# The start of a fused transformer block: g_mix_pre first, the first weights in pieces, and zeros through TensorE until they are there

## The chip, the cores and the metric

One core of one Trainium2 chip runs the whole kernel. The metric is the device time in microseconds (us) of one execution, the median over runs.

## The reference, cut to what matters

One layer of a hybrid block on `x` of 1024 tokens by 1024 channels, all in float32:

```python
h = rmsnorm(x, g_mix_pre)                       # x * rsqrt(mean(x*x) + eps) * g
proj = h @ w_in                                 # 1024 x 3592
qa, ka, va, gate_a, beta_a, alpha_a, qb, kb, vb = split(proj)
out_a = gated_deltanet(qa, ka, va, gate_a, beta_a, alpha_a, ...)
out_b = dilated_attention(qb, kb, vb, rel_bias)
x = x + rmsnorm(concat(out_a, out_b) @ w_out, g_mix_post)
h = rmsnorm(x, g_ffn_pre)
x = x + rmsnorm((silu(h @ w_gate) * (h @ w_up)) @ w_down, g_ffn_post)
```

The change lies in the loads and the first products of `proj = h @ w_in`. The kernel multiplies `x * g` by the weights and puts the factor `rsqrt(mean(x*x) + eps)` of a token on the result.

## The kernel before, in words

Every float32 matrix operand is split in two: a rounded high part `hi` (float32r, cast by ScalarE) and the rest `lo = x - hi` (VectorE). A product is three matmuls (`mm3`): hi by hi, hi by lo, lo by hi. Names that end in `h` and `l` (`hTh`, `hTl`) are these two parts.

The work is written as strands: Python generators that yield one operation after the other. A planner (`Weaver`) picks at each step the operation that its own cost table lets start first, and so writes out one fixed order for each engine before the chip sees anything. On the chip each engine keeps its order and waits on semaphores. So a change in what a strand yields, or in when the planner believes data to be there, can move other instructions. An `After` request makes a strand wait in the planner's clock until the tile was written; a `Get` waits for a free buffer.

The part at issue, in the program's order:

- **Weights.** `load_w` issues loads on SyncE's queue (SP). `w_in` lies in 128-column chunks; a chunk goes to two tiles `wr` of four k tiles each (256 KB). Four buffers `wr` exist. `prep_w` casts and subtracts (`split_sb`) each to tiles `w`.
- **x, transposed.** `load_xt(k, hf)` loads 128 channels (k tile k of 8) by 512 tokens (half hf) to `xT` (256 KB, six buffers); `prep_xt` multiplies by the column of `gT` (the transposed `g_mix_pre`, 4 KB) on ScalarE (`hTh`) and VectorE (`hTl`).
- **x, by tokens.** `load_x(t)` loads 128 tokens by 1024 channels to `xn` (512 KB, three buffers). `norm_in` sums the squares on ScalarE (the instruction that writes `junk`), then VectorE (`n_m`) and GpSimd (`rtok`) make the factor of each token. The fourth `xn` load needs the buffer of the first, and so waits for the first sum of squares; the eighth waits for the fifth's. For every four token tiles, four TensorE transposes against `ident` turn `rtok` into a row, which ScalarE copies to `rb`. The fourth of these transposes needs the fourth `rtok`.
- **TensorE.** `main` runs `proj_first(hf)`, 48 matmuls of 128x512 (8 k tiles, two chunks: `k0` and `q0` in the list `ORDER`, three each) into two banks `pj`, and then `proj_v(0, ...)` for four token tiles: 24 matmuls of 128x264 each into banks `tp`. First hf = 0 with token tiles 0 to 3, then hf = 1 with 4 to 7, then the next chunks (`proj_half`).

Loads leave SP in this order: weights and xT of half 0, `wba`, the four tiles for `proj_v`, `ident`, four `xn`, eight `xT` of half 1, four more `xn`, further weights.

Of the kernel before, what the change touches and what calls it, by code (L numbers as in the profile page):

```python
# [11 lines left out]
F32 = mybir.dt.float32  # L12
# [200 lines left out]
class After:  # L213


    def __init__(self, *aps, late=0.0):
        self.aps, self.late = aps, late


class Strand:  # L220
# [16 lines left out]
class Weaver:  # L237
# [125 lines left out]
    def run(self, *until):  # L363
        while not all(e.set for e in until):
            live, moved = [], True
            while moved:
                moved, live = False, []
                for s in list(self.strands):
                    old = s.req
                    if self.step(s):  # L370
                        live.append(s)
                    if s.req is not old:
                        moved = True
                if self.fresh:
                    self.fresh, moved = False, True
            if all(e.set for e in until):
                break
            assert live, [(s.gen.__name__, s.gen.gi_frame.f_lineno, s.req.__class__.__name__) for s in self.strands]
            first = 1e30
            for s in live:  # L380
                if s.alts is not None:
                    s.req = s.alts[0]
                    if s.ver >= 0:
                        s.req = min(s.alts, key=lambda r: self.finish(s, r, live))
                names = [x.tensor.name for x in s.req.aps] if isinstance(s.req, After) else \
                    [x[0] for op in s.req for x in op.ins + op.outs]
                v = sum(self.ver.get(n, 0) for n in names)
                if v != s.ver:
                    s.ver = v
                    if isinstance(s.req, After):  # L390
                        s.data = max([t for x in s.req.aps for t, _ in self.wr.get(x.tensor.name, {}).values()] + [0.0])
                    else:
                        s.data = max(self.when(op) for op in s.req)
                if isinstance(s.req, After):
                    s.start, s.safe = s.data + s.req.late, True
                else:
                    free = self.clock[s.req[0].eng]
                    s.start = max(free, s.data, self.port if s.req[0].port else 0.0)
                    if s.req[0].eng == "PE":
                        s.start = max(s.start, self.rest.get(s.gen.__name__, 0.0) if s.pace else 0.0)  # L400
                    if s.req[0].table not in (None, self.table) and not s.eager:
                        s.start += TABLE
                    s.safe = s.req[0].eng != "PE" or s.data + s.slack <= free
                first = min(first, s.start)
            best = min((s for s in live if s.start == first), key=lambda s: s.prio)
            if isinstance(best.req, After):
                best.req = None
                continue
            eng = best.req[0].eng
            same = [s for s in live if not isinstance(s.req, After) and s.req[0].eng == eng]  # L410
            best = min((s for s in same if s.start <= first), key=lambda s: (not s.safe, s.prio))
            start = best.start
            if best.req[0].table is not None:
                start = best.data
            for op in best.req:
                start = max(start, self.clock[eng])
                self.issue(op, start)
            if best.pace and eng == "PE":
                self.rest[best.gen.__name__] = self.clock[eng] + best.pace
            best.req = None  # L420
# [121 lines left out]
def block_kernel(ctx: ExitStack, tc: tile.TileContext, a, out):  # L542
# [23 lines left out]
    def split_sb(hi, lo, src):  # L566
        yield Either(A.copy(hi, src), V.tensor_copy(hi, src), bias=BIAS)
        yield Either(*[e.tensor_tensor(lo, src, hi.bitcast(F32), ALU.subtract) for e in (V, G)])
# [77 lines left out]
    def chunks(item):  # L646
        kind, i = item
        return [24 + 2 * i, 25 + 2 * i] if kind == "bv" else [base[kind] + i]
# [3 lines left out]

    def load_w():

        first = chunks(order[0]) + chunks(order[1])
        got = {c: [] for c in first}
        evs = {c: [Event() for _ in range(2)] for c in first}
        for i in range(2):
            for n, c in enumerate(first):
                wr = yield rawS.get([P, 4, P], F32, name="wr")  # L660
                yield SY.dma_start(wr[:], a["w_in"][c][:, 4 * i:4 * i + 4, :])
                got[c].append(wr)
                evs[c][i].fire()
                if not i:
                    w.spawn(prep_w(c, got[c], evs[c]), 1)
                yield from load_xt(4 * i + n, 0)
                if not i and not n:
                    yield SY.dma_start(gT[:], a["g_mix_pre_t"])
            for k in (2, 3):
                yield from load_xt(4 * i + k, 0)  # L670
        yield SY.dma_start(wba[:], a["w_ba"])
        yield from load_item(order[2])
        yield SY.dma_start(ident[:], a["c_ident"])
        for t in range(4):
            yield from load_x(t)
        for k in range(KT):
            yield from load_xt(k, 1)
        for t in range(4, NT):
            yield from load_x(t)
        ev_x.fire()  # L680
        for item in order[3:]:
            yield from load_item(item)

    def load_item(item):
        for c in chunks(item):
            z, evs = [], [Event() for _ in range(2)]
            for i in range(2):
                wr = yield rawS.get([P, 4, P], F32, name="wr")
                yield SY.dma_start(wr[:], a["w_in"][c][:, 4 * i:4 * i + 4, :])
                z.append(wr)  # L690
                evs[i].fire()
            w.spawn(prep_w(c, z, evs), 1)

    ev_x = Event()
    ev_wh = {(c, i): Event() for c in loaded for i in range(2)}

    def prep_w(c, raw, got):
        hi, lo = [], []
        for i in range(4):
            if c in (24, 25):  # L700
                z = yield wS.get([P, 2, WB], F32R, name="w")
            else:
                z = yield wS.get([P, 4, P], F32R, name="w")
            (lo if i % 2 else hi).append(z)
        wts[c] = hi, lo
        for i, (wh, wl) in enumerate(zip(hi, lo)):
            yield got[i]
            wr = raw[i]
            if c in (24, 25):

                k = 4 * (c - 24) + 2 * i
                yield After(wba[:])
                yield from split_sb(wh[:, :, 256:], wl[:, :, 256:], wba[:, k:k + 2, :])
                wh, wl, wx = wh[:, :, 0:256], wl[:, :, 0:256], wr[:].rearrange("p (k x) c -> p k (x c)", x=2)
            else:
                wh, wl, wx = wh[:], wl[:], wr[:]
            yield After(wr[:])
            yield from split_sb(wh, wl, wx)
            rawS.put(wr)
            ev_wh[c, i].fire()  # L720
        loaded[c].fire()

    def proj_first(hf, sinks):

        cs = chunks(order[0]) + chunks(order[1])
        ps = []
        for _ in cs:
            z = yield pj.get([P, 512], F32, name="pj")
            ps.append(z)
        for k in range(KT):  # L730
            for c, z in zip(cs, ps):
                yield ev_wh[c, k // 4]
                yield ev_xt[k, hf]
                wh, wl = wts[c]
                yield mm3(z[:], wh[k // 4][:, k % 4, :], wl[k // 4][:, k % 4, :], *h_of(k, hf * 512, 512),
                          k == 0, k == KT - 1)
        if hf:
            wS.slots = wS.slots[:8]
            for c in cs:
                wS.put(*wts[c][0], *wts[c][1])  # L740
        return [w.spawn(sink(hf, z), 1) for sink, z in zip(sinks, ps)]
# [554 lines left out]
    with ExitStack() as s0:  # L1296
# [10 lines left out]
        def prep_xt(k, hf, x):  # L1307
# [5 lines left out]
            px.put(x)  # L1313
            ev_xt[k, hf].fire()

        def load_x(t):
            x = yield px.get([P, D], F32, name="xn", bufs=3)
            yield SY.dma_start(x[:], a["x"][t * P:(t + 1) * P, :])
            done_in.append(w.spawn(norm_in(t, x), 1))

        def norm_in(t, x):
# [7 lines left out]
            if t % 4 == 3:  # L1329
# [6 lines left out]
                pt.put(tp)  # L1336
                ev_rb[t // 4].fire()

        w.spawn(issue(V.memset(mhalf[:], -0.5)), 0)
        wS.more(px, "pw", 8)  # L1340
        w.spawn(load_w(), 2)
# [1110 lines left out]
```

## Time and profile before

| | us |
|---|---|
| median of 3 runs | 1224.42 (1222.09 to 1224.97) |
| profiled execution | 1225.21, span 1223.4 |
| TensorE busy | 1203.1 (98% of the span) |
| VectorE, ScalarE, GpSimd busy | 884.5, 546.3, 157.3 |
| first real matmul starts | 5.82 |
| first 48 matmuls (half 0) end and `proj_v` begins | 20.16 |
| half 1 begins, ends | 32.25, 43.13 |
| third group of 128x512 matmuls begins | 55.62 |

Starts are counted from the start of the span; 1.8 us of the profiled execution's own time lie outside the span. In a timeline row the first number is the start, the second the length (of several instructions in a row together), and the bracket says how long the engine stood idle and what ended that. A matmul's length holds its way through the array, so two neighbours overlap; the distance of starts is what one costs. `SPq` rows are DMA issues on SyncE's queue: their length holds the time that the queue waited before it could issue.

### The profile page before, as it was taken

To read this page: it belongs to the slowest core of one execution; us is meant where nothing else is said; L and a number is where in the kernel's file an instruction comes from. 1 tells how busy PE (TensorE), PEld (TensorE's weight loads), DVE (VectorE), ACT (ScalarE), POOL (GpSimd) and SP (SyncE) were. 2 spreads that over 40 slices of the span, in tenths; PEclk is the share of its full clock that TensorE was granted. 3 is DMA by queue.
4 is the path that set the end of the run, shared out by engine and by line. 5 is a ranking of instruction groups with operands and counts; after the bars stand their busy time and mean duration, and the time that the engine had idled before them with its cause. 6 is when DMAs were issued, how large, how long until landed. Compare 5 with 4: busy or idle time off the path is not lost.

```text
span 1223.4 us, 19593 instructions
## 1 busy us (share of the span) xinstructions
PE 1203.1 (98%) x7135; PEld 998.1 (82%) x7135; DVE 884.5 (72%) x1627; ACT 546.3 (45%) x1063; POOL 157.3 (13%) x138
## 2 busy tenths in 40 slices
PE   8999999999999999899999999999999999999997
PEld 6878798788888778788788888888888888888886
DVE  4689969646665756666998876877668767876886
ACT  6655521226665654454643323333333334544541
POOL 0143411001111100001100110111001100000111
PEclk9999999999999999899999999999999999999999
DMA  7655363667546355674544433322343239645335
GB/s 266 207 148 168 104 181 105 135 230 243 188 148 208 106 169 170 217 231 146 183 154 139 138 112 130 120 82 83 104 129 121 74 108 321 229 138 147 103 121 206
DMA packets 152887, 193.03 MB, mean 158 GB/s; under 512 B 29992, under 2 KB 78376, under 8 KB 152792
## 3 DMA queue, kind: packets, MB, share of 16 engines
q1 hardware_dynamic: 148568, 189.69, 48.2%
q10 hardware_dynamic: 4224, 2.10, 0.6%
q8 instruction: 56, 0.92, 0.3%
q14 instruction: 39, 0.32, 0.1%
HBM read 135.88 MB, written 59.66 MB: 160 GB/s over the span
## 4 chain that ended last, share of the span: by engine, by line
PE 83%; DMA 5%; DVE 5%; ACT 2%; issue 2%; SPq 1%; POOL 1%; DVEq 0%; POOLq 0%; ACTq 0%
PE bank L286 47%; PE pj L286 21%; PE tp L286 4%; PE p L286 3%; PE pw L286 3%; PE pS L286 2%; PE pV L286 2%; PE pm L286 2%; DVE yc L286 1%; DMA xn<-in_x 1%; SPq L286 1%; DMA h2l<-d_h 1%; DVE x L286 1%; ACT junk L286 1%; DMA views<-in_w_down 0%
## 5 line engine op out<-in xcount | busy, mean ns | idle before, releaser
L286 PE MATMUL pj<-hTh,w 128*128 128x512 f32 x768 | 264.1, 405 | 5.8 <-ACT hTh L286 5.8
L286 PEld LDWEIGHTS pj<-hTh,w 128*128 128x128 f32 x768 | 145.5, 189 | 40.5 <-ACT hTh L286 5.8
L286 ACT CAST wbh<-wraw 128x512 fp32r<-128x512 f32 x130 | 80.3, 621 | 199.0 <-PE bank L286 123.8
L286 PE MATMUL pj<-hTl,w 128*128 128x512 f32 x384 | 151.2, 394 | 0.0
L286 DVE TENSOR_TENSOR wbl<-wraw,wbh 128x512 fp32r<-128x512 f32 x131 | 92.2, 706 | 29.2 <-ACT wbh L286 29.0
L286 PE MATMUL bank<-views 128*128 128x512 f32 (+1 forms) x307 | 84.8, 384 | 0.0
L286 PEld LDWEIGHTS pj<-hTl,w 128*128 128x128 f32 x384 | 73.0, 190 | 12.6 <-DVE hTl L286 0.7
L286 PE MATMUL bank<-views,dah 128*128 128x512 f32 (+1 forms) x214 | 73.5, 379 | 0.0
L286 PE MATMUL bank<-dbh,views 128*128 128x512 f32 (+1 forms) x201 | 70.3, 380 | 0.0
L286 PEld LDWEIGHTS bank<-views 128*128 128x128 f32 x307 | 57.5, 188 | 11.4
L286 POOL TENSOR_TENSOR m<-m,m 128x512 f32<-128x512 f32 x18 | 28.3, 1573 | 253.2 <-DVE r L286 179.6
L286 PE MATMUL pw<-woh,mh 128*128 128x512 f32 x128 | 52.9, 413 | 3.5 <-ACT mh L286 3.4
L286 ACT CAST w<-wr 128x512 fp32r<-128x512 f32 x53 | 32.5, 617 | 52.2 <-PE pj L286 46.8
L286 PE MATMUL pw<-woh,ml 128*128 128x512 f32 x128 | 51.0, 398 | 0.0
L286 PE MATMUL pw<-wol,mh 128*128 128x512 f32 x128 | 50.9, 398 | 0.0
L286 PE MATMUL bank<-dbh,dah 128*128 128x512 f32 (+1 forms) x129 | 49.1, 381 | 0.0
L286 DVE TENSOR_TENSOR w<-wr,w 128x512 fp32r<-128x512 f32 x44 | 30.6, 702 | 24.9 <-ACT w L286 23.3
L286 DVE SCALAR_TENSOR_TENSOR yc<-raw,convw,yc 128x1024 f32<-128x1024 f32 x36 | 46.5, 1292 | 0.5
L286 PEld LDWEIGHTS bank<-views,dah 128*128 128x128 f32 x214 | 40.0, 188 | 7.7
L286 PEld LDWEIGHTS bank<-dbh,views 128*128 128x128 f32 x201 | 37.7, 188 | 7.1
L286 DVE TENSOR_TENSOR m<-bank,m 128x512 f32<-128x512 f32 x44 | 30.1, 685 | 18.1 <-PE bank L286 18.0
L286 ACT ACTIVATE Sr<-Sr,mx 128x384 f32<-128x384 f32 (+3 forms) x64 | 38.1, 597 | 6.3 <-DVE mx L286 5.9
(377 smaller groups left out, 3058.1 us busy)
## 6 DMA issues: line engine op xcount, KB each, us to landing
wr<-in_w_in SPq DMA_DIRECT2D x56, 256.0 KB
wraw<-in_w_gate SPq DMA_DIRECT2D x52, 256.0 KB
wraw<-in_w_up SPq DMA_DIRECT2D x52, 256.0 KB
views<-d_hid SPq DMA_DIRECT2D x47, 256.0 KB
db<-in_w_down SPq DMA_DIRECT2D x40, 256.0 KB
da<-d_hid SPq DMA_DIRECT2D x30, 256.0 KB
d_hid<-x SPq DMA_DIRECT2D x22, 256.0 KB
d_hid<-r SPq DMA_DIRECT2D x22, 256.0 KB
```

What stands on the lines that cost most here:

```text
L286: op.fn(*op.args, **op.kw)
```

## The change

`load_w` loads `gT` before all else. For the two first chunks a weight tile is loaded in two pieces of two k tiles (128 KB each), in the order: k0 piece, xT, q0 piece, xT, and again for each two k tiles. `prep_w` casts and subtracts by piece; there is one event per piece, and `proj_first` waits for the piece that it needs. `After` can look at a part of a tile. A new strand `warm` clears half of `junk` on VectorE and runs ten matmuls of bf16 zeros, 128x512, into a `tp` bank that is given back.

```diff
     def load_w():
 
+        yield SY.dma_start(gT[:], a["g_mix_pre_t"])
         first = chunks(order[0]) + chunks(order[1])
         got = {c: [] for c in first}
-        evs = {c: [Event() for _ in range(2)] for c in first}
-        for i in range(2):
+        evs = {c: [[Event() for _ in range(2)] for _ in range(2)] for c in first}
+        for k in range(0, KT, 2):
+            i, j = k // 4, k % 4
             for n, c in enumerate(first):
-                wr = yield rawS.get([P, 4, P], F32, name="wr")
-                yield SY.dma_start(wr[:], a["w_in"][c][:, 4 * i:4 * i + 4, :])
-                got[c].append(wr)
-                evs[c][i].fire()
-                if not i:
+                if not j:
+                    wr = yield rawS.get([P, 4, P], F32, name="wr")
+                    got[c].append(wr)
+                yield SY.dma_start(got[c][i][:, j:j + 2, :], a["w_in"][c][:, k:k + 2, :])
+                evs[c][i][j // 2].fire()
+                if not k:
                     w.spawn(prep_w(c, got[c], evs[c]), 1)
-                yield from load_xt(4 * i + n, 0)
-                if not i and not n:
-                    yield SY.dma_start(gT[:], a["g_mix_pre_t"])
-            for k in (2, 3):
-                yield from load_xt(4 * i + k, 0)
+                yield from load_xt(k + n, 0)
...
     def prep_w(c, raw, got):
...
-            yield After(wr[:])
-            yield from split_sb(wh, wl, wx)
+            for j, ev in enumerate(got[i]):
+                yield ev
+                x = (slice(None), slice(2 * j, 2 * j + 2) if len(got[i]) > 1 else slice(None))
+                yield After(wx[x], part=len(got[i]) > 1)
+                yield from split_sb(wh[x], wl[x], wx[x])
+                ev_wh[c, 2 * i + j].fire()
             rawS.put(wr)
-            ev_wh[c, i].fire()
...
-                yield ev_wh[c, k // 4]
+                yield ev_wh[c, k // 2]
...
+        def warm():
+            yield V.memset(junk[:, 0:512], 0.0)
+            tp = yield pt.get([P, 4, P], F32, name="tp")
+            yield [mm(tp[:].rearrange("p k j -> p (k j)"), junk[:, 0:P], junk[:, 0:512]) for _ in range(10)]
+            pt.put(tp)
...
+        w.spawn(warm(), 0)
         w.spawn(issue(V.memset(mhalf[:], -0.5)), 0)
```

Since the planner sees other times, it also writes other orders for the first part of the program. Behind that part the orders are the same but for the numbers in names. Three places of the new orders:

SP at the very start, before:

```order
L286 DMA wr<-in_w_in 128x512
L286 DMA xT<-in_x_t 128x512
L286 DMA gT<-in_g_mix_pre_t 128x8
L286 DMA wr<-in_w_in 128x512
L286 DMA xT<-in_x_t 128x512 x3
```

and after (`128x8` is `gT`, `128x256` a piece of a weight tile):

```order
L286 DMA gT<-in_g_mix_pre_t 128x8
L286 DMA wr<-in_w_in 128x256
L286 DMA xT<-in_x_t 128x512
L286 DMA wr<-in_w_in 128x256
L286 DMA xT<-in_x_t 128x512
```

`gT` moved from third to first, and a piece of each chunk stands ahead of each two x tiles' second.

ScalarE where half 0 ends, before (`ss0` to `ss3` are the sums of squares of token tiles 0 to 3, `raw<-pj` the copies out of the two banks of half 0):

```order
L286 COPY raw_149<-pj_157 128x512
L286 CAST w_252<-wr_244 128x2x256
L286 COPY raw_150<-pj_158 128x512
L286 ACTIVATE junk_155,ss0_268<-xn_260 128x1024
L286 ACTIVATE junk_155,ss1_274<-xn_267 128x1024
L286 ACTIVATE vs_340<-tp_311,rtok_96 128x256
L286 ACTIVATE bp_129<-tp_311,rtok_96 128x8
L286 ACTIVATE junk_155,ss2_279<-xn_273 128x1024
L286 ACTIVATE vs_387<-tp_339,rtok_96 128x256
L286 ACTIVATE junk_155,ss3_345<-xn_326 128x1024
```

and after:

```order
L286 CAST w_277<-wr_270 128x2x256
L286 ACTIVATE junk_155,ss0_292<-xn_286 128x1024
L286 COPY raw_149<-pj_156 128x512
L286 ACTIVATE junk_155,ss1_298<-xn_291 128x1024
L286 COPY raw_150<-pj_157 128x512
L286 ACTIVATE junk_155,ss2_306<-xn_297 128x1024
L286 ACTIVATE junk_155,ss3_339<-xn_328 128x1024
L286 ACTIVATE hTh_108<-xT_338,gT_154 128x512
L286 ACTIVATE hTh_108<-xT_344,gT_154 128x512
L286 ACTIVATE vs_383<-tp_336,rtok_96 128x256
```

The first sum of squares moved ahead of the first copy out of a bank, and all four ahead of the first `vs`.

TensorE around the second group of transposes of `rtok`, before (`pj` rows belong to half 1, `tp` rows to `proj_v` of token tile 4):

```order
L286 MATMUL pj_479<-hTl_111,w_175 128x512
L286 MATMUL pj_479<-hTh_110,w_176 128x512
...
L286 MATMUL tp_578<-w_231,hTh_108 128x264
L286 MATMUL tp_578<-w_232,hTh_108 128x264
L286 MATMUL tp_578<-w_231,hTl_109 128x264
L286 MATMUL tp_592<-ident_66,rtok_96 128x128 x4
L286 MATMUL tp_578<-w_250,hTh_110 128x264
```

and after:

```order
L286 MATMUL pj_515<-hTh_110,w_169 128x512
L286 MATMUL pj_515<-hTl_111,w_169 128x512
L286 MATMUL pj_515<-hTh_110,w_170 128x512
L286 MATMUL tp_587<-ident_66,rtok_96 128x128 x4
L286 MATMUL pj_516<-hTh_110,w_187 128x512
...
L286 MATMUL pj_516<-hTh_110,w_188 128x512
L286 MATMUL tp_614<-w_247,hTh_108 128x264
```

These transposes moved from behind the 12th matmul of token tile 4 to behind the 39th of the 48 matmuls of half 1, so 21 matmuls earlier. The first group moved as well: it stood behind 78 of the 96 matmuls of `proj_v` for token tiles 0 to 3, and stands behind 54 of them now.

More of the change, by code (lines that the diff above doesn't have):

```diff
@@ L213, with __init__ @@
 class After:
-    def __init__(self, *aps, late=0.0):
-        self.aps, self.late = aps, late
+    def __init__(self, *aps, late=0.0, part=False):
+        self.aps, self.late, self.part = aps, late, part
 class Strand:
@@ L390, in run @@
                     if isinstance(s.req, After):
-                        s.data = max([t for x in s.req.aps for t, _ in self.wr.get(x.tensor.name, {}).values()] + [0.0])
+                        own = [self.region(x) if s.req.part else (x.tensor.name, -1, -1) for x in s.req.aps]
+                        s.data = max([t for n, q, f in own for (p, g), (t, _) in self.wr.get(n, {}).items() if p & q and f & g] + [0.0])
                     else:
@@ L685, in load_item @@
         for c in chunks(item):
-            z, evs = [], [Event() for _ in range(2)]
+            z, evs = [], [[Event()] for _ in range(2)]
             for i in range(2):
@@ L690, in load_item @@
                 z.append(wr)
-                evs[i].fire()
+                evs[i][0].fire()
             w.spawn(prep_w(c, z, evs), 1)
     ev_x = Event()
-    ev_wh = {(c, i): Event() for c in loaded for i in range(2)}
+    ev_wh = {(c, i): Event() for c in loaded for i in range(4)}
     def prep_w(c, raw, got):
@@ L706, in prep_w @@
         for i, (wh, wl) in enumerate(zip(hi, lo)):
-            yield got[i]
+            yield got[i][0]
             wr = raw[i]
```

## The prediction

> **What bounds the kernel now.** The page gives TensorE 98% of the span. I then read TensorE's waits over the whole kernel; only 20 us are idle, and the groups that matter here are these (wait, total, times, longest).
>
> ```profile
> PE 1203.1 (98%) x7135; PEld 998.1 (82%) x7135; DVE 884.5 (72%) x1627; ACT 546.3 (45%) x1063; POOL 157.3 (13%) x138
> ...
> PE pj L286 <- ACT hTh L286: 5.8, 1, 5.8
> PE pw L286 <- ACT mh L286: 3.4, 1, 3.4
> ...
> PE pm L286 <- DVE rhd L286: 1.0, 1, 1.0
> ...
> PE tp L286 <- POOL rtok L286: 0.2, 1, 0.2
> ```
>
> The 5.8 us wait is the start. The timeline shows what it waits for, and a second loss that counts as busy: TensorE is slow at first.
>
> ```profile
> 0.74 0.40 SPq L286 DMA_DIRECT2D wr<-in_w_in  x1
> 1.20 0.41 SPq L286 DMA_DIRECT2D xT<-in_x_t  x1
> 1.65 0.43 SPq L286 DMA_DIRECT2D gT<-in_g_mix_pre_t  x1
> ...
> 3.48 0.62 ACT L286 CAST w<-wr 128x512 fp32r<-128x512 f32 x1 [1.46 <-DMA wr<-in_w_in]
> ...
> 5.04 0.72 ACT L286 ACTIVATE hTh<-xT,gT 128x512 fp32r<-128x512 f32 x1 [0.95 <-DMA gT<-in_g_mix_pre_t]
> ...
> 5.82 0.80 PE L286 MATMUL pj<-hTh,w 128*128 128x512 f32 x1 [5.82 <-ACT hTh L286]
> ...
> 10.05 1.05 PE L286 MATMUL pj<-hTh,w 128*128 128x512 f32 x2
> 10.91 0.63 PE L286 MATMUL pj<-hTl,w 128*128 128x512 f32 x1
> ...
> 19.25 0.62 PE L286 MATMUL pj<-hTh,w 128*128 128x512 f32 x2
> 19.70 0.39 PE L286 MATMUL pj<-hTl,w 128*128 128x512 f32 x1
> ...
> 20.16 0.41 PE L286 MATMUL tp<-w,hTh 128*128 128x264 f32 x2
> ...
> 29.62 0.60 PE L286 MATMUL tp<-ident,rtok 128*128 128x128 f32 x4
> ...
> 32.25 0.39 PE L286 MATMUL pj<-hTh,w 128*128 128x512 f32 x1
> ...
> 43.13 0.41 PE L286 MATMUL tp<-w,hTh 128*128 128x264 f32 x2
> ...
> 45.26 0.32 PE L286 MATMUL tp<-ident,rtok 128*128 128x128 f32 x1 [0.17 <-POOL rtok L286]
> 45.34 0.49 PE L286 MATMUL tp<-w,hTh 128*128 128x264 f32 x2
> ...
> 55.62 0.39 PE L286 MATMUL pj<-hTh,w 128*128 128x512 f32 x1
> ...
> 152.45 0.73 PE L286 MATMUL pm<-rhd,tgtr 128*128 128x512 f32 x2 [0.99 <-DVE rhd L286]
> ```
>
> Two starts of 128x512 are 0.86 us apart at 10.05 (0.43 each) and 0.45 us apart at 19.25 (0.23 each). So the 48 matmuls of half 0 take 14.34 us (5.82 to 20.16), while the same 48 of half 1 take 10.88 (32.25 to 43.13; 0.227 each): 3.46 us are lost to the slow clock and to gaps. A 128x264 costs 9.46 / 78 = 0.121 (20.16 to 29.62) or 10.28 / 84 = 0.122 (45.34 to 55.62).
>
> The row at 45.26 is the important one. TensorE waits only 0.17 us there for the eighth `rtok`, but it waits: something else arrives at the same time as TensorE. The chain of waits up to there names it.
>
> ```profile
> 21.16 1.17 ACT junk L286 x2
> ...
> 22.34 0.33 SPq L286
> ...
> 22.71 5.41 DMA xT<-in_x_t
> ...
> 28.15 1.39 ACT hTh L286 x2
> ...
> 29.57 0.75 DVE hTl L286
> ...
> 30.72 6.49 DMA xn<-in_x
> ...
> 37.30 1.16 ACT junk L286 x2
> ...
> 38.47 4.62 DMA xn<-in_x
> ...
> 44.66 0.56 POOL rtok L286
> ...
> 45.26 10.52 PE tp L286 x85
> ```
>
> It is a chain of loads: the first sum of squares (21.16) frees the `xn` buffer for the fourth load (22.34); behind it the xT loads of half 1 go, the last two of which wait for `hTl`; then the fifth `xn` (30.72), whose sum of squares frees the buffer of the eighth (38.47), whose `rtok` TensorE needs. No TensorE work is in it from 21.16 on. From the first sum of squares to the second transposes' end of waiting it is 45.26 - 21.16 = 24.10 us.
>
> **The change, part by part.**
>
> *gT first, pieces.* gT leaves first, so it is no longer last at 5.04; xT is issued third, at about 1.65. Its landing is between 2.7 us after issue (first weight tile, 0.74 to 3.48) and 3.3 (gT, 1.65 to 5.0): 4.4 to 5.0, so the first real matmul could start 0.78 later, at 5.2 to 5.8. Four casts and four subtractions more fall on ScalarE and VectorE; between no cost (the data is the same) and 8 x 0.62, they lie beside a TensorE that needs 10.9 us for what these engines do in less, and cost nothing; without that cover the last k tile would be late by them.
>
> *Ten zero matmuls.* At the slow 0.43 they take 4.3 us. The clear is short and VectorE idle, so they run from about 1.4 to 5.7, in TensorE's 5.8 us of idleness, and the real ones start at about 5.7. What they are worth is the clock: between nothing (14.34 stays) and all of 3.46. I take 0.8 us left over, since the release need not coincide with 5.7 and the data come one k tile at a time: half 0 ends at 5.7 + 10.88 + 0.8 = 17.4 instead of 20.16, 2.8 earlier. [...]
>
> *Reordered transposes.* Here the gain meets the chain of loads. ScalarE's first sum of squares stood behind the copy out of the bank that TensorE fills last, hence 21.16. Now it stands ahead of it and waits for its load alone. When does that land? These rows bound it.
>
> ```profile
> 13.32 9.35 SPq L286 DMA_DIRECT2D xn<-in_x  x4
> ...
> 16.50:20.00 3.50, 3.50 (x17) 2.88 (x16) 1.20 (x3) 0.74 (x3) 0.00 (x0) 1.00 0.89 325
> 20.00:22.00 2.00, 2.00 (x18) 1.96 (x17) 0.69 (x1) 2.00 (x4) 0.00 (x0) 1.00 0.14 57
> ...
> 26.61 1.05 ACT L286 ACTIVATE junk<-xn 128x1024 bf16<-128x1024 f32 x1
> ...
> 28.02 0.55 POOL L286 TENSOR_TENSOR rtok<-n_m,mhalf 128x1 f32<-128x1 f32 x1 [2.15 <-DVE n_m L286]
> ```
>
> The queue is full up to 20 (last columns: DMA share, GB/s), and 1.5 MB at 325 GB/s are 4.7 us: three `xn` loads move from about 15.4 to 20, the first third until 17.0; but the row of 20 to 22 shows a tail of 2 us, for a load has landed only with its slowest engine. So 17.0 to 20; I take 19.4, near the upper end, for every `xn` here has that tail. The bytes ahead of it are the same as before, so it does not come sooner because TensorE does. The chain moves from 21.16 to 19.45, by 1.7 us.
>
> First transposes: the fourth `rtok` ended at 28.57 and comes at 26.9 at the latest; since the sum at 26.61 had also stood behind a `vs`, I take 26.6. TensorE arrives at 17.4 + 54 x 0.121 = 23.9 and waits 2.7 us. Then 0.36 for the transposes and 42 x 0.121 bring half 1 to 32.05, against 32.25: the lead is gone.
>
> Second transposes: TensorE arrives at 32.05 + 39 x 0.227 = 40.9. The release is 45.26 - 1.7, less 0.33 for one store (`d_v`) that no longer stands between the loads: 43.2. It waits 2.3 us. Behind the transposes there are now 9 x 0.227 + 96 x 0.122 = 13.8 us of work, where 84 x 0.122 = 10.3 stood: the third group begins at 43.2 + 0.08 + 13.8 = 57.1 against 55.62, so 1.5 us later.
>
> *What comes after.* The orders behind are the same and TensorE is busy, so the 1.5 us travel on. VectorE gets `rb` earlier (43.3 against 45.3 for the transposes), so the one wait for VectorE, 0.99 us at 152.45, goes: 0.5 us are left. The wait for `mh` hangs on stores and loads behind TensorE's work and moves along.
>
> Sum against the profiled execution: 1225.21 + 0.5 = 1225.7. That execution lies 0.79 above the median of 1224.42, so in terms of medians: **1224.9 us**.
>
> **The rivals.**
>
> *The loads come in time.* If no engine had a tail, the first `xn` would land at 17.0 and every later load up to 2 us sooner; TensorE would not wait and the third group would begin 17.4 + 35.46 = 52.9, 2.8 us earlier: 1221.7. For it: tails differ from run to run. Against it: the chain has four such loads in a row and must lose 5 us, not 2. And VectorE, which ends the wait at 152.45, would have to come forward as well.
>
> *The clock falls again in the new wait (slower).* One row shows what a long wait does: TensorE idles from 493.8, and the granted clock (PEclk) is half for 6.8 us.
>
> ```profile
> 493.80:496.90 3.10, 0.42 (x2) 0.00 (x0) 3.09 (x5) 1.65 (x5) 0.40 (x1) 1.00 0.75 234
> 496.90:503.70 6.80, 6.09 (x16) 4.83 (x17) 3.02 (x6) 1.24 (x4) 0.56 (x1) 0.50 0.58 165
> ```
>
> Half a clock for the 6.1 busy us costs 3.0. At the first transposes this would be half hidden (2.3 us of slack before the second). At the second nothing hides it: if that wait grows from 2.3 to the 3.4 us of this row, the time is 0.5 + 1.1 + 3.0 = 4.6 over: 1229. It decides at 1.1 us more tail. [...]
>
> *The zeros do not lift the clock.* Half 0 would end at about 20, TensorE would reach the first transposes at 26.5, just when they are released, and all that follows is as forecast: 1224.9. The forecast does not need the lift.
>
> **How the numbers follow.** About 0.3% (3.7 us) is what a measurement of this kernel tells from no change. Forecast (a small loss, hidden gain) 0.62, zeros without effect 0.08 (same time), loads in time 0.20, clock falls 0.10. Loads in time reaches below 1220.7 in a third of its cases, and other clock waits spread by a few us, so faster by over 0.3%: 0.09; slower 0.13 with the tails of the forecast; within 0.78. The range leaves out the slow rival and the lower half of the fast one: 1221.2 to 1228.3. The forecast's own is 1223 to 1227.5.
>
> **What would show it.** Right: zeros from about 1.4; 128x512 starts 0.23 apart by 9; half 0 done near 17.4; waits of 2 to 3 us on `rtok` at about 24 and 41; half 1 near 32; the third group near 57. Wrong, and how: no wait on `rtok` and the third group before 54 (loads in time, the steps "first third until 17.0" and "24.10" fail); a granted clock of 0.5 near 27 or 43; half 0 done at 20.

## The result and the profile after

The change makes the kernel slower: 1227.55 us (median of 6 runs, 1226.74 to 1228.61) against 1223.26 (6 runs, 1221.72 to 1224.97) for the kernel before, a ratio of 1.0035 with a 95% interval of 1.0022 to 1.0048. The loss is 4.3 us. The forecast was 1224.9, a loss of 0.5 us and so no measurable change. The measured time lies inside the stated range (1221.2 to 1228.3) and 0.05 us above the forecast's own (1223 to 1227.5). The profiled execution took 1226.74, with a span of 1225.0.

TensorE's waits in the profile after (total, times, longest) show that the 5.8 us at the start are gone (1.2 us ahead of the zeros, put down to `mhalf`, are left of them) and that new waits for `rtok` stand in their place:

```profile
PE tp L286 <- POOL rtok L286: 3.6, 3, 1.6
...
PE tp L286 <- DVE mhalf L286: 1.2, 1, 1.2
PE pm L286 <- DVE rhd L286: 1.0, 1, 1.0
```

TensorE's timeline after, at the places that the prediction names:

```profile
1.25 3.84 PE L286 MATMUL tp<-junk 128*128 128x512 bf16 x10 [1.25 <-DVE mhalf L286]
...
5.13 0.49 PE L286 MATMUL pj<-hTh,w 128*128 128x512 f32 x1
...
17.83 0.41 PE L286 MATMUL tp<-w,hTh 128*128 128x264 f32 x2
...
24.39 0.38 PE L286 MATMUL tp<-ident,rtok 128*128 128x128 f32 x2
25.81 0.32 PE L286 MATMUL tp<-ident,rtok 128*128 128x128 f32 x1 [1.03 <-POOL rtok L286]
27.68 0.32 PE L286 MATMUL tp<-ident,rtok 128*128 128x128 f32 x1 [1.55 <-POOL rtok L286]
...
34.47 0.39 PE L286 MATMUL pj<-hTh,w 128*128 128x512 f32 x1
...
43.33 0.49 PE L286 MATMUL tp<-ident,rtok 128*128 128x128 f32 x3
44.83 0.32 PE L286 MATMUL tp<-ident,rtok 128*128 128x128 f32 x1 [1.01 <-POOL rtok L286]
...
58.70 0.39 PE L286 MATMUL pj<-hTh,w 128*128 128x512 f32 x1
```

Half 0 ends at 17.83 instead of 20.16, and the third group of 128x512 matmuls begins at 58.70 instead of 55.62. In 41 us a lead of 2.3 us has become a lag of 3.1. The chain of waits of the kernel after says what the second transposes (at 44.83) waited for: the same loads as before.

```profile
15.23 5.41 DMA xn<-in_x
...
22.91 5.33 DMA xT<-in_x_t
...
30.66 5.18 DMA xn<-in_x
...
37.10 5.40 DMA xn<-in_x
...
45.15 2.07 PE pj L286 x9
47.22 11.64 PE tp L286 x96
```

The last two rows are the work that now stands behind the transposes: 9 matmuls of half 1 and all 96 of `proj_v`, 58.70 - 44.83 = 13.87 us. Before, it was 55.62 - 45.26 = 10.36.

### The profile page after: what moved, and what is told of

Its sections match the earlier page's. It is cut to its first block, busy times and chain, and to the rows that moved or that the text cites. A ratio compares the mean times of both kernels' runs of the same rounds, so it can differ in the third digit from the quotient of the medians.

```text
span 1225.0 us, 19632 instructions
## 1 busy us (share of the span) xinstructions
PE 1204.5 (98%) x7145; PEld 998.5 (82%) x7145; DVE 884.9 (72%) x1634; ACT 545.9 (45%) x1065; POOL 157.9 (13%) x138
## 4 chain that ended last, share of the span: by engine, by line
PE 87%; DVE 4%; DMA 3%; issue 2%; ACT 1%; SPq 1%; POOL 1%; DVEq 0%; POOLq 0%; ACTq 0%
PE bank L286 50%; PE pj L286 20%; PE pw L286 5%; PE tp L286 4%; PE p L286 3%; PE pS L286 2%; PE pV L286 2%; PE pm L286 2%; DMA xn<-in_x 1%; DVE yc L286 1%; DMA xT<-in_x_t 1%; SPq L286 1%; DVE x L286 0%; DMA d_gt<-gst 0%; DMA wraw<-in_w_gate 0%
## 5 line engine op out<-in xcount | busy, mean ns | idle before, releaser
L286 ACT CAST w<-wr 128x512 fp32r<-128x512 f32 (+1 forms) x55 | 32.1, 586 | 52.2 <-PE pj L286 47.1
L286 DVE TENSOR_TENSOR w<-wr,w 128x512 fp32r<-128x512 f32 (+1 forms) x48 | 31.4, 658 | 21.8 <-ACT w L286 19.2
```

What stands on the lines that cost most here:

```text
L286: op.fn(*op.args, **op.kw)
```

## The experiments

The kernels ran on three chips. The kernel before had medians there of 1223.57 (zeros_only to priced), 1223.26 (priced_late to before_late) and 1223.60 (the rest), and each ratio is against its runs on the same chip. All numbers of a timeline are of one profiled execution. In the table "half 0 ends" is the first matmul of `proj_v`, "reached" the first and "released" the last of the second group of transposes, and "third group" the 128x512 matmuls after that.

| kernel | median | ratio (95%) | half 0 ends | reached | released | third group | from release |
|---|---|---|---|---|---|---|---|
| before | 1223.26 | | 20.16 | 44.60 | 45.26 | 55.62 | 10.36 |
| after | 1227.55 | 1.0035 (1.0022 to 1.0048) | 17.83 | 43.33 | 44.83 | 58.70 | 13.87 |
| zeros_only | 1227.13 | 1.0029 (1.0016 to 1.0042) | 18.48 | 41.80 | 44.24 | 59.49 | 15.25 |
| loads_only | 1223.46 | 1.0007 (0.9998 to 1.0015) | 18.76 | 43.20 | 45.15 | 55.49 | 10.34 |
| order_only | 1224.81 | 1.0015 (1.0006 to 1.0025) | 19.23 | 40.28 | 42.21 | 56.76 | 14.55 |
| priced | 1224.29 | 1.0002 (0.9993 to 1.0011) | 17.75 | 43.21 | 46.68 | 58.54 | 11.86 |
| priced_late | 1220.26 | 0.9975 (0.9963 to 0.9986) | 17.96 | 48.20 | | 54.46 | |
| zeros_late | 1220.58 | 0.9982 (0.9970 to 0.9995) | 19.27 | 48.08 | | 54.34 | |
| loads_late | 1221.04 | 0.9980 (0.9968 to 0.9991) | 18.16 | 47.14 | | 53.40 | |
| before_late | 1221.80 | 0.9987 (0.9976 to 0.9997) | 18.11 | 46.92 | | 53.18 | |
| after_filled | 1227.72 | 1.0039 (1.0026 to 1.0053) | 18.29 | 43.13 | 45.00 | 58.87 | 13.87 |

The theory that they test: ten zeros stand in the planner's books with 0.853 us each, 8.5 us in all, while the chip takes 3.84 for the ten. The planner therefore believes TensorE to be late, places the transposes of `rtok` ahead of 21 matmuls that stood ahead of them, and TensorE meets them before the chain of `xn` loads releases them. Behind them then lies more work, and the chain sets when it starts. The rivals: the load order itself costs (pieces, a different queue), or the clock, which falls again in the new wait, does.

**Which part: zeros_only.** The kernel before with `warm` alone.

```diff
+        w.spawn(warm(), 0)
         w.spawn(issue(V.memset(mhalf[:], -0.5)), 0)
```

> The kernel before with the ten zero matmuls alone; gT, weights and x load as before. Theory (order): the planner books 0.85 us for each zero, the trace after shows 0.38; so it believes TensorE late and puts the transposes of rtok early, here behind 48 of the 96 matmuls of proj_v and behind 33 of the 48 of half 1. TensorE then waits for rtok twice, and the third group of 128x512 matmuls begins at about 58.7 us (release about 43.6, then 15 x 0.227 + 96 x 0.122 = 15.1), 3 us later than before: slower by 2 to 5 us. Rival (loads): the pieces and gT first are what costs, since the first xn load landed later; without them the zeros are a pure gain: half 0 ends near 17.8 instead of 20.2 and the time falls by 1 to 3 us.

Measured: 1227.13, as slow as the whole change. Its timeline:

```profile
13.30 8.06 SPq L286 DMA_DIRECT2D xn<-in_x  x4
...
28.32 0.32 PE L286 MATMUL tp<-ident,rtok 128*128 128x128 f32 x1 [2.88 <-POOL rtok L286]
...
44.24 0.32 PE L286 MATMUL tp<-ident,rtok 128*128 128x128 f32 x1 [1.95 <-POOL rtok L286]
...
59.49 0.39 PE L286 MATMUL pj<-hTh,w 128*128 128x512 f32 x1
```

Here the planner puts the first transposes behind 48 of the 96 matmuls and the second behind 33 of the 48 of half 1, so still earlier than in the change. The release at 44.24 is no later than before, but 15.25 us of work stand behind it. The loss does not need the new loads. A part of it goes with the granted clock: that averages 0.9958 over the 12 runs and 0.9965 over before's 35 on this chip, and 0.0008 of 1225 us is, as an estimate, 1.0 us.

**loads_only.** The change without `warm`; its transposes stand where they stood before.

```diff
-        w.spawn(warm(), 0)
         w.spawn(issue(V.memset(mhalf[:], -0.5)), 0)
```

> The change without the zeros: gT first and weights in pieces. The orders on TensorE, ScalarE and SP around the transposes are those of before (behind 78 of 96, and behind 12 of proj_v's tile 4). Theory (order): no early transposes, so no loss: the first real matmul starts at about 5.2, the clock rises late as before, half 0 ends at 19 to 20, the third group begins at 54.5 to 56.5; within 1.5 us of before. Rival (loads): the later xn loads alone cost it, third group near 58.5, slower by 3 to 4 us.

Measured: 1223.46, no difference.

```profile
15.15 6.77 SPq L286 DMA_DIRECT2D xn<-in_x  x4
...
45.15 0.32 PE L286 MATMUL tp<-ident,rtok 128*128 128x128 f32 x1 [1.46 <-POOL rtok L286]
...
55.49 0.39 PE L286 MATMUL pj<-hTh,w 128*128 128x512 f32 x1
```

TensorE is 1.4 us earlier at the transposes than in before's profile (43.20 against 44.60) and gives all of it back in a wait of 1.46. This is the plainest case of the change's fate: a gain ahead of a chain of loads is worth nothing until the chain moves. The first row is the rival's trace: `xn` loads are issued at 15.15 instead of 13.32. It delays the chain, but at the price of no measurable time here.

**order_only.** The kernel before; only the planner's TensorE clock is set 8.535 us later at the start, and no instruction is added.

```diff
+        w.clock["PE"] += 10 * 853.5
         w.spawn(issue(V.memset(mhalf[:], -0.5)), 0)
```

> The kernel before without any zeros and with its own loads; only the planner's clock of TensorE starts 8.5 us later, as the ten zeros had moved it. No instruction is added or removed. The transposes stand behind 54 of 96 matmuls of proj_v and behind 36 of 48 of half 1, and ScalarE's sums of squares ahead of the copies out of the banks. Theory (order): TensorE starts as before (5.8, slow clock, half 0 done near 20), waits for rtok at the transposes, third group near 58 (release about 43.5 to 44, then 12 x 0.227 + 96 x 0.122 = 14.4): slower by 2 to 4 us. Rival (loads): no change, within 1 us.

Measured: 1224.81, slower by 0.15% (0.06 to 0.25): the sign is right, the size smaller than expected.

```profile
42.21 0.32 PE L286 MATMUL tp<-ident,rtok 128*128 128x128 f32 x1 [1.44 <-POOL rtok L286]
...
56.76 0.39 PE L286 MATMUL pj<-hTh,w 128*128 128x512 f32 x1
```

14.55 us lie behind the release, as in the change, but the release comes at 42.21, earlier than in any other profile here in which TensorE waits for it: its `xn` loads leave SP at 13.11, its first sum of squares starts at 19.65, and its eighth `xn` is issued at 34.74 (before: 38.47). So a false price alone, without any zeros, makes the kernel slower; what it costs is (work behind) + (release), and both must be read.

**priced.** The whole change, with the zeros booked at the 0.384 us that they take. The transposes return to their old places (behind 78, and behind the 12th of token tile 4).

```diff
-            yield [mm(tp[:].rearrange("p k j -> p (k j)"), junk[:, 0:P], junk[:, 0:512]) for _ in range(10)]
+            ops = [mm(tp[:].rearrange("p k j -> p (k j)"), junk[:, 0:P], junk[:, 0:512]) for _ in range(10)]
+            for op in ops:
+                op.cost = 384.0
+            yield ops
```

> The whole change, but the planner books 0.384 us (the measured distance) for each zero instead of 0.853. The program issues the same operations; the transposes go back to where they stood before. Theory (order): half 0 ends near 17.8, the first transposes are reached at 27.3 and wait under 0.7 us, half 1 runs from 30 to 41, the second transposes are reached at 42.3 and wait 1 to 2.5 us for the chain of xn loads; third group at 54 to 55.5: faster than before by 0.5 to 2 us, and 4 to 6 us faster than the change. Rival (loads): as slow as the change, 3 to 4 us above before.

Measured: 1224.29, equal to before (0.9993 to 1.0011). One number in the planner takes away the loss, but the gain that I expected does not appear. (ScalarE's order goes back together with the transposes, so this run does not part the two. That the transposes make the loss is read from the work that stands behind them, 13.87 us in the change and 10.35 in before.) Its timeline and a window of it (length, then busy time with counts of TensorE, weight loads, VectorE, ScalarE, GpSimd, then the granted clock) show where it goes:

```profile
46.68 0.32 PE L286 MATMUL tp<-ident,rtok 128*128 128x128 f32 x1 [2.98 <-POOL rtok L286]
```

```profile
43.90:47.30 3.40, 0.62 (x5) 0.62 (x6) 1.18 (x3) 2.71 (x6) 0.55 (x1) 1.00 0.73 231
47.31:50.73 3.42, 3.42 (x18) 3.42 (x17) 3.32 (x6) 2.07 (x5) 0.00 (x0) 0.50 0.72 179
```

TensorE arrives at 43.21, 1.4 us before it did in before's profile, and waits 2.98, and in this execution the clock falls behind the wait: 11.86 us for what takes 10.35 at full clock. This profiled execution (1226.69) is the longest of the kernel's 11 runs (1221.74 to 1226.69) and so not a typical one. Over the 11 runs the granted clock averages 0.9963, against 0.9965 before, so the clock is not what holds back the median; in the execution shown, the wait eats the lead.

**Holding the transposes back: priced_late.** If the release binds and nothing soon needs the row `rb`, the transposes can wait longer than the loads do. An event lets the second group start only behind 48 of the 96 matmuls of `proj_v`; the first stays behind 78.

```diff
+    ev_go = {3: Event(), 6: Event()}
...
         for t in tiles:
+            if not m and t in ev_go:
+                ev_go[t].fire()
...
+                yield ev_go[3 if t == 3 else 6]
                 yield After(rtok[:, t - 3:t + 1], ident[:])
```

> The whole change with the zeros booked at 0.384 us, and the second transposes of rtok held back until 48 of the 96 matmuls of proj_v of half 1 are done (before: 12; the first stay behind 78). Theory (chain of xn loads): their release stays at 42 to 47 us whatever TensorE does, as in all six profiles so far (42.2 to 46.7); TensorE now reaches them at about 47 and does not wait, so the early start is kept at last: third group of 128x512 matmuls at 52.5 to 54 instead of 55.6, faster than before by 1.5 to 3 us. Rival (the loads are too slow for an early start, something else than the transposes stops TensorE, such as the xT tiles of half 1 or a bank of proj_v): another wait takes its place, third group at 55 or later, no faster than before.

Measured: 1220.26, a ratio of 0.9975 (0.9963 to 0.9986): faster than both kernels, by the medians 3.0 us under before and 7.3 under the change.

```profile
48.20 0.60 PE L286 MATMUL tp<-ident,rtok 128*128 128x128 f32 x4
...
54.46 0.39 PE L286 MATMUL pj<-hTh,w 128*128 128x512 f32 x1
```

All four transposes go through in one row, without a wait, and the third group begins 1.16 us before that of before's profile and 4.2 before the change's. It is later than the expected 52.5 to 54: at the first transposes, which are not held back, TensorE still waits 0.80 us. Against the mean of three executions of before (54.90, see the repeats) it is only 0.44 us earlier.

So the third group does not account for the gain of 3.0 us, and the rest of this one execution is the clock. In all three profiles of before the clock falls behind the wait for `mh` near 495 us and stays at half for 6.83 us; here it does not fall (1.00 in the third column from the right):

```profile
495.25:498.66 3.41, 2.47 (x10) 1.70 (x11) 2.55 (x6) 0.89 (x3) 0.56 (x1) 1.00 0.84 256
```

From the first matmul behind that wait to the end of the span it is 725.8, 725.7 and 724.2 us in before's executions and 722.2 here, 3.0 less than their mean; up to that matmul the lead is 0.7 (496.19 against 496.93 on average). Over all runs the clock is not the gain: it averages 0.9970 in the 12 runs and 0.9968 in before's 35, and runs at the same clock still differ, by 3.0 us at 0.997 (means of 1219.90 in 6 runs and 1222.87 in 9) and by 1.8 at 0.996 (1222.46 in 4 and 1224.26 in 14). The gain stands; where all of it is made, this profile does not show.

**zeros_late, loads_late, before_late.** The same held-back transposes with the zeros alone (priced right), with the loads alone, and as a control without either.

> The loads of before, the zeros alone booked at 0.384 us, and the second transposes held back as in priced_late. Theory (chain): the zeros bring half 0's end from 20.2 to about 18, and it is kept: third group at 53 to 54.5, faster by 1 to 2.5 us; against priced_late it shows what the loads part is worth (0 to 0.7 us). Rival: no faster than before.

> gT first and weights in pieces without the zeros, second transposes held back. Theory (chain): TensorE starts at 5.2 and half 0 ends 0.5 to 1.4 us before that of before, kept: third group at 54 to 55.2, faster by 0.4 to 1.6 us. Rival (the pieces and the later xn loads cost by themselves): third group at 55.6 or later.

> Control: the kernel before with the second transposes held back and nothing else. Theory (chain): TensorE waits only 0.17 us for them there, so holding them back gains 0.2 us at most: third group at 55.3 to 55.7, same time within 0.5 us. Rival (the place of the transposes is worth something by itself, for the work behind them on ScalarE and VectorE): it differs by more than 1 us, slower if VectorE is now late with the first chunks.

Measured: 1220.58, 1221.04 and 1221.80. The third groups of the last two (53.40 and 53.18) come earlier than expected, and the control was a miss in its time too: it is faster than before by 1.5 us where I expected 0.5 at most. Its TensorE rows, and then VectorE's `rhd` in before (first) and in the control:

```profile
46.92 0.60 PE L286 MATMUL tp<-ident,rtok 128*128 128x128 f32 x4
...
53.18 0.39 PE L286 MATMUL pj<-hTh,w 128*128 128x512 f32 x1
```

```profile
150.69 1.71 DVE L286 TENSOR_TENSOR rhd<-g,mDT 128x1024 fp32r<-128x1024 f32 x1
```

```profile
145.92 1.22 DVE L286 TENSOR_TENSOR rhd<-g,mDT 128x1024 fp32r<-128x1024 f32 x1
```

In all four held-back kernels TensorE's wait of 1.0 us for `rhd` near 152 is gone. In the control's order VectorE's instructions stand otherwise, with this `rhd` ahead of a reduction that it followed before, and it takes 1.22 us where it took 1.71. So up to 1.0 of the control's 1.5 us can be a side effect of holding back. The wait for `rtok` itself was 0.17, 0.29 and nothing in the three executions of before, too little for the rest, which stays open. What zeros and loads are worth once the second transposes do not wait would be the step from the control to priced_late, 1221.80 to 1220.26: 1.5 us, and the zeros or the loads alone lie between. The intervals of these four ratios overlap, so this order among them is not shown, and the single profiles do not follow it (the control's profiled execution was the shortest of its 12 runs). That the side effect on VectorE is 1.0 was read from the profiles and not tried by itself, and it need not last: in priced_late a wait of 1.91 us for `mh` near 489 (at most 0.42 in before's three) gives a lead back.

**Is it the clock? after_filled.** The change, with ten matmuls that multiply data already at hand placed directly ahead of the first transposes, so that TensorE is not idle there.

```diff
-                yield [tr(tp[:, i, :], rtok[:, t - 3 + i:t - 2 + i].broadcast_to([P, P])) for i in range(4)]
+                z = hT[0, 0][0]
+                ops = [mm(tp[:].rearrange("p k j -> p (k j)"), z[:, 0, 0:P], z[:, 0, :]) for _ in range(10 if t == 3 else 0)]
+                for op in ops:
+                    op.cost = 1.0
+                yield ops + [tr(tp[:, i, :], rtok[:, t - 3 + i:t - 2 + i].broadcast_to([P, P])) for i in range(4)]
```

> The change with ten more matmuls (128x512, their result is overwritten by the transposes) right ahead of the first transposes of rtok, where TensorE waited 1.0 and 1.55 us and the granted clock then fell to half from 28.2 to 31.7. The order is otherwise that of the change. Theory (chain of xn loads): the clock no longer falls, half 1 begins 1 to 1.5 us earlier (about 33 instead of 34.5), but the second transposes are released at 44 to 45 as before, so TensorE waits 2 to 3 us there instead of 1.3, and the third group still begins at 58 to 59.5: within 1 us of the change's 1227.5. Rival (the fallen clock is what costs): third group near 57.3, 1.5 us faster than the change.

Measured: 1227.72, the time of the change. First two windows of the change, then one of the filled kernel, then the latter's timeline:

```profile
24.80:28.20 3.40, 0.84 (x5) 0.66 (x6) 1.05 (x3) 1.90 (x5) 1.10 (x2) 1.00 0.95 301
28.20:31.70 3.50, 3.50 (x19) 3.50 (x18) 2.45 (x5) 3.43 (x7) 0.42 (x1) 0.51 0.85 265
```

```profile
28.20:31.70 3.50, 2.97 (x22) 2.76 (x23) 2.14 (x3) 3.20 (x6) 0.35 (x1) 1.00 0.97 337
```

```profile
45.00 0.32 PE L286 MATMUL tp<-ident,rtok 128*128 128x128 f32 x1 [1.38 <-POOL rtok L286]
...
58.87 0.39 PE L286 MATMUL pj<-hTh,w 128*128 128x512 f32 x1
```

In the change the clock falls to half behind the first transposes and 128x264 matmuls start 0.22 apart instead of 0.12; in the filled kernel it stays at 1.00. The time is the same, for the second release (45.00) is set by loads. One part of the expectation missed: half 1 begins at 34.27, hardly before the change's 34.47 and not at about 33, because the ten matmuls put the last of the first transposes at 28.61 instead of 27.68, and the second wait is 1.38, not 2 to 3. So TensorE did not come earlier here, and what the run shows is that the loss is there with the clock at full: over its five runs the clock averages 0.9968, before's nine on this chip 0.9967, and 4.1 us are lost all the same. The fall at the first transposes is not what the change costs.

**Repeats: before_again, before_again2, after_again.** One execution each, profiled, of the unchanged kernels.

> The kernel before, unchanged, for a second profile. Theory (chain): the clock's release and the first landing differ from one execution to the next, and where TensorE starts earlier than in the first profile it waits longer at the second transposes: half 0 done at 18 to 20, a wait of 0.2 to 2.2 us for rtok, third group at 54.5 to 56 all the same. Rival (TensorE's start sets the time): the third group moves with the start, no longer wait.

> The kernel before, unchanged, a third profile, with the same expectation as the second: third group at 54.5 to 56 wherever half 0 ends; and the clock falls again behind the wait for mh near 494 us for 3.4 or 6.8 us.

> The change, unchanged, for a second profile. Theory (chain): release of the second transposes at 43 to 46.5, third group 13.8 to 14.1 us behind it, so at 57 to 60.5, whether or not the clock falls at the first transposes.

Measured: 1223.86, 1222.74 and 1229.46. The three fences are in this order:

```profile
43.80 0.60 PE L286 MATMUL tp<-ident,rtok 128*128 128x128 f32 x4
...
54.41 0.39 PE L286 MATMUL pj<-hTh,w 128*128 128x512 f32 x1
```

```profile
44.31 0.32 PE L286 MATMUL tp<-ident,rtok 128*128 128x128 f32 x1 [0.29 <-POOL rtok L286]
...
54.66 0.39 PE L286 MATMUL pj<-hTh,w 128*128 128x512 f32 x1
```

```profile
45.95 0.32 PE L286 MATMUL tp<-ident,rtok 128*128 128x128 f32 x1 [2.03 <-POOL rtok L286]
...
59.83 0.39 PE L286 MATMUL pj<-hTh,w 128*128 128x512 f32 x1
```

Over three executions of before the third group begins at 54.90 on average (55.62, 54.41, 54.66), over two of the change at 59.27 (58.70, 59.83): 4.37 later, against 4.29 between the medians. From there to the end of the span it is 1167.2 us on average before and 1167.0 in the change. So the whole loss is made in the first 60 us. It has two terms: the work behind the last of the second transposes, 13.87 against 10.35, makes 3.5; the start of that transpose, 45.39 against 44.55 on average (45.26, 44.31, and 44.07 for the last of the four in the row at 43.80, which start 0.09 apart), makes 0.8.

The expectation for the kernel before missed in part. In before_again TensorE did not wait for `rtok` at all, and the third group came at 54.41, just ahead of the range: it moved with TensorE's start, as the rival had it. The three executions show why. In before, the first sum of squares stands behind the copy out of the bank that half 0 fills last, and it starts 1.00 us behind the end of half 0 each time (21.16, 20.36, 20.09 after 20.16, 19.36, 19.09). So the chain of loads moves with TensorE there. In the change it hangs on the first `xn` load alone. The clock fell behind the wait for `mh` in both repeats of before, as expected, for 6.83 us.

## Why the prediction was right or wrong, point by point

*Zeros and half 0: near, by two errors against each other.* The zeros ran from 1.25 to 5.1, and half 0 ended at 17.83, forecast 17.4. But the first real matmul came at 5.13, not 5.7, and half 0 took 12.70 us, not 10.88 + 0.8: the leftover was 1.8. In the change this is not the clock, which was granted at 4.35. The first eight matmuls take 3.53 us (5.13 to 8.66) where 8 x 0.227 = 1.8 would do, since they come one by one as `hTl` and `hTh` get done (waits of 0.29, 0.19 and 0.28); and in the repeat, with the clock granted only at 7.17, half 0 took 12.75. Also, the gain was measured against 20.16, and that was a late execution: the repeats of before end half 0 at 19.36 and 19.09. Against the mean of the three, 19.54, the lead is 1.7 us, not 2.8.

*Two waits on `rtok`, work behind the second: right; half 1's start: wrong.* TensorE reached the first transposes at 24.39 (23.9 forecast) and waited 2.58 us in two pieces (2.7). The work behind the second took 13.87 (13.8). Between them half 1 began at 34.47 and not at 32.05: the fourth `rtok` came at 27.68 instead of 26.6, and the 42 matmuls behind it took 6.79 us instead of 5.1, partly at half the clock. It cost nothing more, because the second release came later still: TensorE waited 1.01 there (2.03 in the repeat; 2.3 forecast).

*"So 17.0 to 20; I take 19.4 ... The bytes ahead of it are the same as before": wrong, the first `xn` landed at 20.6 (15.23 + 5.41), in the repeat at 21.1.* This is the term that failed first. The prediction asked what the pieces cost TensorE and found nothing. It did not ask what SP's queue waits for. Here is VectorE in the kernel before, and then SP, VectorE and ScalarE in the kernel after:

```profile
11.75 0.68 DVE L286 TENSOR_TENSOR w<-wr,w 128x512 fp32r<-128x512 f32 x1
12.36 2.08 DVE L286 SCALAR_TENSOR_TENSOR hTl<-xT,gT,hTh 128x512 fp32r<-128x512 f32 x3
```

```profile
10.54 4.16 SPq L286 DMA_DIRECT2D wr<-in_w_in  x4
...
13.93 0.42 DVE L286 TENSOR_TENSOR w<-wr,w 128x256 fp32r<-128x256 f32 x1
14.26 0.74 DVE L286 SCALAR_TENSOR_TENSOR hTl<-xT,gT,hTh 128x512 fp32r<-128x512 f32 x1
...
15.23 7.01 SPq L286 DMA_DIRECT2D xn<-in_x  x4
...
20.74 1.06 ACT L286 ACTIVATE junk<-xn 128x1024 bf16<-128x1024 f32 x1 [1.69 <-DMA xn<-in_x]
```

The four `wr` loads ahead of `xn` need the four `wr` buffers, and the last is free only when the last piece is subtracted, at 13.93 + 0.42 = 14.35 (before: 12.43). The issue of `xn` moves from 13.32 to 15.23. The added work is the smaller part of that: VectorE ends its work for half 0 at 15.00 instead of 14.44, 0.6 us later. The rest is the place of the last piece. Before, three `hTl` stood behind the last subtraction; now one does, and the other two come ahead of it. The loads part does this: first issues at 15.15 with it alone, 13.30 with the zeros alone. There the first sum of squares started at 19.86, so 19.4 had been a good estimate of a load without the delay. The bytes were the same; the time from which they could be loaded was not.

*Release of the second transposes: mis-sized, 45.39 instead of 43.2.* 1.3 to 1.75 us of it are the late first `xn` (20.74 and 21.20 for the sum of squares, against 19.45). The rest is the length of the chain from there, taken as 23.8: it was 24.1 and 24.75 in the two executions of the change, and 22.6 to 25.8 over all the kernels here whose second transposes wait. It was a range, and I used one value. These 2.2 us explain the third group: 57.1 + 2.2 = 59.3.

*"So the one wait for VectorE, 0.99 us at 152.45, goes": wrong.* The waits show it unchanged at 1.0. VectorE's timeline after:

```profile
153.76 1.72 DVE L286 TENSOR_TENSOR rhd<-g,mDT 128x1024 fp32r<-128x1024 f32 x1
```

In before this `rhd` started at 150.69 and took 1.71: it moved by 3.07, the lag of TensorE at that point. VectorE there works on TensorE's products and follows it; `rb` had long been there (its second copy ended at 45.78, 45.19 + 0.59). I argued from when an input of VectorE comes without reading what it waits for at that place.

*The level.* The forecast added its difference to the profiled execution and took 0.79 off for the median of three runs. The repeats show that execution 0.7 late at the third group already. The loss then reads: 0.5 forecast, 2.2 for the release, 1.0 for `rhd`, 0.7 for the late reference, 4.4 in all; 4.3 was measured.

*The rivals.* The loads did not come in time. The clock did fall, at the first transposes, and as the prediction had it, that place is hidden: the filled kernel is no faster. Zeros without effect did not happen, but the remark behind it holds for the change: as long as the chain hangs on loads, the time does not depend on when half 0 ends. (In before it does, as the repeats show.) A loss above 0.3% was given a chance of 0.13, and it came, with 0.35%. The bounds of the release (tails of up to 2 us on each of four loads) reached as far, but the sum took one value for each. That 1227.55 still lies inside the stated range is owed to the width of the range, not to the sum: the loss of 4.3 us was forecast as 0.5.

## What to carry to other kernels

Ask of a gain at the start which load, by way of which buffer, next holds the engine, and count the buffers' release in the queue's own order: a tile that is worked on in pieces is free only behind its last piece, and where that stands in the order can delay the loads behind it though the busy engine loses nothing (here the issue of `xn` went from 13.32 to 15.23). Where a planner writes the order, an instruction that it prices wrongly moves others; the price of the added work belongs to the change (here, with 0.853 us per zero the change loses 4.3 us against the kernel before, and with 0.384 it loses 0.7, which is within the noise). And place an instruction that waits for a load late, if its result is not needed soon: what stands behind a wait is paid from the release on (here 13.87 us instead of 10.35).

## What was not expected of the hardware

In these profiles the clock's falls followed a grid, not the length of the wait. In the records of the granted clock every period after the first release, but for the last, which the end of the program cuts off, is a multiple of 3.41 us (23.89, 3.41 and 471.04 in the change's profile; 484.69, 6.83 and 716.80 in before's). The change lost the clock behind a stretch with waits of 1.03 and 1.55; zeros_only kept it through waits of 0.43 and 2.88. Its windows, cut at its own grid, show the difference:

```profile
23.06:26.47 3.41, 1.94 (x15) 1.51 (x13) 0.15 (x1) 1.35 (x4) 0.55 (x1) 1.00 0.99 290
26.47:29.88 3.41, 1.56 (x13) 1.56 (x14) 1.76 (x4) 3.41 (x8) 0.55 (x1) 1.00 0.70 263
```

The grid line at 26.47 splits the idle time, and each half has over 1.5 us of work (1.94 and 1.56); the change's window of 24.80 to 28.20 lies within 0.04 us of its grid and has 0.84. Over 14 profiles, up to 87 us and from 470 to 527 us, 15 of the 16 falls came behind a grid window with 0.20 to 1.51 us of TensorE work, and no such window kept the clock at under 1.53 (one fall came behind 2.04). The prediction let the clock fall at the second transposes if TensorE's wait there grew to the 3.4 us of the wait for `mh`. That limit was my estimate from this one wait, and no run shows it: in the change the clock fell behind waits of 1.03 and 1.55.

The first release varies likewise: with zeros running from 1.25 in every case, the clock was granted at 4.35 in the change's profile and at 7.17 in its repeat, and half 0 still ended at 17.83 and 17.88.
